# Strips stored by ScalarE, a corner block stored twice, and gate products moved into a loop

## The chip, the cores and the metric

One core of one Trainium2 chip runs the whole kernel. The engines are TensorE (PE in the profile, its weight loads PEld), VectorE (DVE), ScalarE (ACT), GpSimd (POOL) and SyncE (SP, which here only issues DMAs). The metric is the device time of one execution in microseconds, the median of several runs.

## The reference, cut to what matters

One decoder layer on 1024 tokens of width 1024, in float32:

```python
f1 = swiglu(rms_norm(h, ffn1_pre_g), ffn1_w_in, ffn1_w_out)
h = h + 0.5 * rms_norm(f1, ffn1_post_g)
u = rms_norm(h, mix_pre_g)
p_rwkv, p_swa, q_mem, gate_logits = split(u @ w_in)
y_a = rwkv7_mix(p_rwkv, ...)                 # linear recurrence over time, 8 heads of 64
y_b = sliding_window_gqa_sinks(q, k, v, sinks)
y_c = memory_cross_attention(q_mem, mem_n, mem_w_kv)
g = sigmoid(gate_logits + gate_b)            # three gates of width 1024
merged = sum(g_i * (y_i @ w_branch_i))
h = h + rms_norm(merged @ w_out, mix_post_g)
f2 = swiglu(rms_norm(h, ffn2_pre_g), ffn2_w_in, ffn2_w_out)
h = h + 0.5 * rms_norm(f2, ffn2_post_g)
```

The change lies in the middle: in `rwkv7_mix`, whose recurrence runs in chunks of 64 tokens, and in the columns of `u @ w_in` that give the queries, keys and gates.

## The kernel before, in words

Every large product is exact float32 made of three matmuls on split operands (high times high, high times low, low times high; `mm3`, lines 374 to 379). ScalarE casts a weight to its high part (`w_hi`, L300), VectorE subtracts to get the low part (`w_lo`, L302), from a raw tile (`w_raw`) that SP loads (L291). Eight operands are made ahead.

The mixer runs through these stages, each with other work laid between its matmuls:

- **Preparation** (`rwkv_prep`, 700 to 890 us in the profile). For each of four pairs of heads it projects r, k and v, applies the token shift (`raw` tiles, whose first eight columns POOL clears, L970; L965 and L966 mix), and forms the decays. `gram` (L1105) computes, for each half of the sixteen chunks, a 64 by 64 matrix per chunk and head: 128 of them in all. VectorE masks them into a tile `ab` (L1116; one buffer), and SP stores them to `ab_d` (L1118). `ss` and `rk` are sums over a head's channels by matmul (L993).
- **Inverse** (`rwkv_invert`). All 128 matrices are loaded, one per partition, and VectorE inverts the two diagonal 32 by 32 blocks of each; the result goes to `inv_d`, the transpose of one of the blocks to `turn_d`.
- **Pairs of strips** (`win_pair`, L1407). Meanwhile PE computes seven pairs of column strips of `u @ w_in`, each with seven half-size products in place of eight (sums of the operands stand in `mix_form`). Three PSUM banks px, py, pz collect the products. `made` adds a kept sum to a bank and writes half a strip (`att`, L1433; a gate strip's Tanh is L1436). After the seventh product SP stores both strips of 512 KB (L1455): six to `att_d`, eight to `gate_d`.
- **Corner** (`rwkv_corner`, L1167). The off-diagonal 32 by 32 block of each inverse is the product of three blocks: `up` (from `ab_d`), `turned` and `low` (from `inv_d`). SP loads each with four DMAs in pieces of 128 bytes; eight groups of small matmuls (L1185) stand between the products of pairs 4 and 5. ScalarE stores the result into `inv_d` (L1191).
- **Chain** (`rwkv_chain`, L1201). Sixteen chunks in sequence. `f` and `dinv` of a chunk are loaded from `pk_d` and `inv_d` (`chunk_fetch`). In an iteration PE computes z from the state sv, the outputs y, the solution z times dinv, the next chunk's values and gram, the new state and a transpose bkt; VectorE and ScalarE copy between. Products of gate blocks (`pgate`) fill PE's waits. Blocks 10 and 11 (`gate_block`) come whole, the later ones from a generator (`filling`), from which `fill(n, behind)` takes n matmuls that may not start before `behind`.
- **Finish** (`rwkv_finish`). The group norm: for each of eight half-rows a square by ScalarE (`ysq_hi`), its low part by VectorE (`ysq_lo`), a sum by PE (`var`, L1337) and a logarithm by ScalarE (`yrs`), then exponentials. Tanh of the gates needs another table on ScalarE than logarithm and exponential; ACT_TABLE_LOAD switches.

What sets the order on each engine is a scheduler that goes by priorities: `high_priority(offset=...)` moves a group ahead (`lead` 300, `urgent` 1000), `issue_after` holds one back, and `keep_in_program_order` fixes matmuls among themselves. Each engine then runs its own list in order, and a DMA waits in its queue in order as well.

Of the kernel before, what the change touches and what calls it, by code (L numbers as in the profile page):

```python
# [11 lines left out]
F32 = mybir.dt.float32  # L12
# [6 lines left out]
P = 128  # L19
# [19 lines left out]
NPAIR = 4  # L39
# [10 lines left out]
CORNER = (4, 4)  # L50
# [42 lines left out]
class Block:  # L93
# [6 lines left out]
    def mm(self, *args, start=True, stop=True):  # L100
        return self.k.tc.keep_in_program_order(self.nc.tensor.matmul(*args, start=start, stop=stop))
# [130 lines left out]
class Builder:  # L232
# [768 lines left out]

    def rwkv_prep(self, u, pool, pk_d, ab_d, bonus_d, att_d):
        nc = self.nc
# [51 lines left out]
        for p in range(NPAIR):  # L1055
# [49 lines left out]
            def gram(p=p, at=at, bk=bk, bka=bka):  # L1105
                store(bka, 0, p)

                for half in (0, 1):
                    ps = self.psum("ab")
                    for c in range(8):  # L1110

                        for rows, q in heads[::-1]:
                            cc = half * 8 + c
                            keep(nc.tensor.matmul(ps[rows, c * C : (c + 1) * C], bk[q][rows, cc], at[rows, cc], start=True, stop=True))
                    ab = pool.tile([P, 8, C], F32, tag="ab", name="ab", bufs=1)
                    V.tensor_tensor(ab, ps.rearrange("p (c t) -> p c t", t=C), self.gmask[:, 0:1, :].broadcast_to([P, 8, C]), ALU.mult)  # L1116
                    for q in (0, 1):
                        nc.sync.dma_start(ab_d[half * 8 : (half + 1) * 8, p, q].rearrange("c s t -> s c t"), ab[q * 64 : q * 64 + 64])  # L1118

            def bonus(p=p, parts=m_parts, m=m, rv=rv, v=v):  # L1120
# [45 lines left out]

    def rwkv_corner(self, pool, ab_d, inv_d, turn_d):  # L1167

# [5 lines left out]
        with urgent():  # L1174
            for t, d in ((up, flat(ab_d)[:, :H, H:]), (turned, turn_d), (low, flat(inv_d)[:, H:, H:])):
                for g in groups:
                    nc.sync.dma_start(t[g], d[g].rearrange("i s t -> s i t"))
        for w, x, out in ((up, turned, half), (half, low, corner)):
# [22 lines left out]
    def rwkv_chain(self, pool, early, fetched, pk_d, inv_d, y):  # L1201
# [23 lines left out]
        def values(n, ps):  # L1225

            for p, q in pairs:
                mm(at(ps, p, 1 - q, W4), n["f"][ROWS[q], p, 4, :], self.center[ROWS[q]])
            for t in ("sv", "uv"):
                for q in (0, 1):  # L1230
                    S.copy(n[t][ROWS[1 - q], q], v3(ps, W4)[ROWS[1 - q]])

        def grams(n):
# [32 lines left out]
        G.memset(n["sv"][hi, 1], 0.0)  # L1266
        values(n, self.psum("y"))
        grams(n)
# [3 lines left out]
        for c in range(NC_):  # L1272
# [15 lines left out]
            for p, q in pairs:  # L1288
                self.solved = mm(at(ps, p, q, W4), n["d"][ROWS[q], p, :], z[ROWS[q], p, :])
            for q in (0, 1):  # L1290
# [116 lines left out]
    def win_pair(self, i, fs, out, att_d, gate_d, between=lambda: None):  # L1407
# [21 lines left out]
        def made(n, t, h, ps, x=None):  # L1429
            t, f = t[:, halves[h]], strips[n]  # L1430
            with self.tc.high_priority(offset=self.lead):
# [5 lines left out]
                elif x is None:  # L1437
                    nc.scalar.copy(t, ps)

        part(0, "b11", px, True)  # L1440
        x = kept(px)
# [8 lines left out]
        part(5, "b22", pz, False, True)  # L1450
        made(0, first, 1, pz, u1)
        part(6, "t4", px, False, True)
        made(1, second, 0, px)
        for f, t in zip(strips, (first, second)):
            nc.sync.dma_start(gate_d[f - 24] if f >= 24 else att_d[ATT_ROW[f]], t)  # L1455

# [284 lines left out]
    def mixer(self, u, cp, close_raws, att_d, gate_d, km_d, vm_d):  # L1741
        nc, tc, io = self.nc, self.tc, self.io
        pk_d = tc.dram_tile([NC_, P, NPAIR, 5 * C], F32, name="pk_d")
        ab_d = tc.dram_tile([NC_, NPAIR, 2, C, C], F32, name="ab_d")
        inv_d = tc.dram_tile([NC_, NPAIR, 2, C, C], F32, name="inv_d")
        turn_d = tc.dram_tile([P, H, H], F32, name="turn_d")
# [9 lines left out]
        with tc.tile_pool(reuse_waits="tile", name="prep", bufs=8) as pool:  # L1756
            self.rwkv_prep(u, pool, pk_d, ab_d, bonus_d, att_d)
        forms = over.enter_context(tc.tile_pool(reuse_waits="tile", name="mix_forms", bufs=1, side="right"))
# [5 lines left out]
        with tc.tile_pool(reuse_waits="tile", name="gates", bufs=2) as gp:  # L1764
# [17 lines left out]
            with tc.tile_pool(reuse_waits="tile", name="corner", bufs=1) as pool:  # L1782
                lumps = itertools.chain(itertools.repeat(None, CORNER[1]), self.rwkv_corner(pool, ab_d, inv_d, turn_d))
                for i in range(CORNER[0], len(WIN_PAIRS) - 1):
                    self.win_pair(i, fs, out, att_d, gate_d, lambda: next(lumps, None))
                assert next(lumps, None) is None
            chunks = contextlib.ExitStack()
            early = chunks.enter_context(tc.tile_pool(reuse_waits="tile", name="chunks", bufs=2))
            fetched = [self.chunk_fetch(early, c, pk_d, inv_d) for c in (0, 1)]
            self.win_pair(len(WIN_PAIRS) - 1, fs, out, att_d, gate_d)  # L1790
            over.close()
            with chunks, tc.tile_pool(reuse_waits="tile", name="chain", bufs=2) as pool:
                y = pool.tile([P, NPAIR, T], F32, name="y", bufs=1)
                last = self.rwkv_chain(pool, early, fetched, pk_d, inv_d, y)
                for g in range(GATES_FIRST, GATES_EARLY):
                    self.gate_block(g, u, gp, gate_d)
                self.held = []
                self.fills, self.missing = self.filling(u, gp, gate_d, y_d), 0
                self.fill(8, self.solved)
                last()  # L1800
# [267 lines left out]
```

## Time and profile before

| | us |
|---|---|
| median of 3 runs | 2256.76 (2256.03 to 2258.38) |
| profiled execution | 2257.27 |
| its span, first to last instruction | 2255.6 |
| TensorE busy | 2227.7 (99%) |
| VectorE / ScalarE / GpSimd busy | 1642.0 / 1028.9 / 58.8 |
| mean granted TensorE clock | 0.997 |

The stages of the change lie between 760 and 1200 us. In the windows each engine's busy time stands with its count of instructions; a window's length less PE's busy time is PE's idle time there. SP's DMAs are listed by issue, not by transfer; POOL issues no DMA before the change.

### The profile page before, as it was taken

Reading aid. Unit: us, or ns where it says so; the run is one execution under the profiler, and the core shown is the slowest. Engines: PE = TensorE matmul, PEld = TensorE weight load, DVE = VectorE, ACT = ScalarE, POOL = GpSimd, SP = SyncE. Lnnn points to the kernel's source line nnn. Section 1 sums busy time; section 2 is a strip of 40 time slices with the busy share of each in tenths; the row PEclk is TensorE's granted clock in tenths of the full one; section 3 lists DMA queues with packets and bytes.
Section 4 is the critical chain, followed back from the end, with each engine's and each line's share of the span. In section 5 each row is a group of like instructions: output and inputs, shape, how many; then the busy total and the mean of one; then the engine's idle time right before and its main releaser. Section 6 shows DMA issues by size and latency. Waiting matters only on the chain.

```text
span 2255.6 us, 34511 instructions
## 1 busy us (share of the span) xinstructions
PE 2227.7 (99%) x12304; PEld 1832.2 (81%) x12304; DVE 1642.0 (73%) x2761; ACT 1028.9 (46%) x1933; POOL 58.8 (3%) x114
## 2 busy tenths in 40 slices
PE   8999999999999999999999999999999999999998
PEld 6888888888887788877878887788888888888887
DVE  6988767766698887863667577794898886656576
ACT  6523333454556654444355454444663223345451
POOL 0000000000000000000330000000000000000000
PEclk9999999999999999999999999999999999999999
DMA  8565666686665356464538877564565552347663
GB/s 292 174 202 169 202 210 214 229 294 205 191 210 188 120 150 204 155 169 153 158 95 276 270 252 250 185 202 142 174 214 176 194 189 100 114 164 249 205 196 121
DMA packets 279132, 431.90 MB, mean 191 GB/s; under 512 B 58512, under 2 KB 96912, under 8 KB 278704
## 3 DMA queue, kind: packets, MB, share of 16 engines
q1 hardware_dynamic: 266160, 409.96, 56.0%
q10 hardware_dynamic: 12800, 19.73, 2.7%
q8 instruction: 97, 1.59, 0.3%
q14 instruction: 75, 0.61, 0.1%
HBM read 292.75 MB, written 135.79 MB: 190 GB/s over the span
## 4 chain that ended last, share of the span: by engine, by line
PE 51%; DMA 1%; DVE 1%; ACT 1%; issue 0%; SPq 0%; DVEq 0%; ACTq 0%
PE px L377 4%; PE px L379 4%; PE px L378 4%; PE po L377 3%; PE po L378 3%; PE po L379 3%; PE pgate L377 2%; PE pgate L378 2%; PE pgate L379 2%; PE pz L377 2%; PE pz L379 2%; PE pz L378 2%; PE pb L377 2%; PE pb L378 2%; PE pb L379 2%; PE pw L378 1%
## 5 line engine op out<-in xcount | busy, mean ns | idle before, releaser
L300 ACT CAST w_hi<-w_raw 128x512 fp32r<-128x512 f32 x608 | 376.2, 620 | 725.0 <-PE px L378 189.9
L302 DVE TENSOR_TENSOR w_lo<-w_raw,w_hi 128x512 fp32r<-128x512 f32 x608 | 417.3, 688 | 191.0 <-ACT w_hi L300 171.7
L379 PE MATMUL po<-u,w_lo 128*128 128x512 f32 (+1 forms) x476 | 180.9, 380 | 0.0
L378 PE MATMUL po<-u,w_hi 128*128 128x512 f32 (+1 forms) x476 | 180.9, 380 | 0.0
L377 PE MATMUL po<-u,w_hi 128*128 128x512 f32 (+1 forms) x476 | 180.9, 380 | 0.0
L377 PE MATMUL px<-u,w_hi 128*128 128x512 f32 x380 | 147.9, 389 | 0.8 <-DVE km L1596 0.8
L377 PE MATMUL pz<-u,w_hi 128*128 128x512 f32 x380 | 148.1, 390 | 0.0
L378 PE MATMUL px<-u,w_hi 128*128 128x512 f32 x380 | 147.9, 389 | 0.0
L379 PE MATMUL px<-u,w_lo 128*128 128x512 f32 x380 | 147.8, 389 | 0.0
L379 PE MATMUL pz<-u,w_lo 128*128 128x512 f32 x380 | 147.8, 389 | 0.0
L378 PE MATMUL pz<-u,w_hi 128*128 128x512 f32 x380 | 147.8, 389 | 0.0
L377 PE MATMUL px<-f,w_hi 128*128 128x512 f32 x352 | 137.1, 390 | 0.0
L379 PE MATMUL px<-f,w_lo 128*128 128x512 f32 x352 | 137.0, 389 | 0.0
L378 PE MATMUL px<-f,w_hi 128*128 128x512 f32 x352 | 136.9, 389 | 0.0
L486 DVE TENSOR_TENSOR u<-hid,u 128x512 fp32r<-128x512 f32 x114 | 78.3, 690 | 44.7 <-ACT u L485 43.7
L378 PEld LDWEIGHTS po<-u,w_hi 128*128 128x128 f32 x476 | 89.5, 188 | 17.2
L379 PEld LDWEIGHTS po<-u,w_lo 128*128 128x128 f32 x476 | 89.5, 188 | 17.0
L377 PE MATMUL pgate<-u,w_hi 128*128 128x512 f32 x256 | 103.3, 403 | 0.0
L377 PEld LDWEIGHTS po<-u,w_hi 128*128 128x128 f32 x476 | 89.5, 188 | 16.8
L378 PE MATMUL pgate<-u,w_hi 128*128 128x512 f32 x256 | 101.0, 395 | 0.0
L485 ACT CAST u<-hid 128x512 fp32r<-128x512 f32 x114 | 70.6, 620 | 65.0 <-DMA hid<-form_d 54.2
L379 PE MATMUL pgate<-u,w_lo 128*128 128x512 f32 x256 | 100.3, 392 | 0.0
(453 smaller groups left out, 5162.1 us busy)
## 6 DMA issues: line engine op xcount, KB each, us to landing
w_raw<-in_ffn_in SPq DMA_DIRECT2D x224, 256.0 KB
hid<-form_d SPq DMA_DIRECT2D x154, 256.0 KB
w_raw<-in_win SPq DMA_DIRECT2D x112, 256.0 KB
form_d<-g SPq DMA_DIRECT2D x88, 256.0 KB
w_raw<-ffn_sum_d SPq DMA_DIRECT2D x88, 256.0 KB
form_d<-h SPq DMA_DIRECT2D x66, 256.0 KB
w_raw<-in_ffn_out SPq DMA_DIRECT2D x66, 256.0 KB
first_d<-first SPq DMA_DIRECT2D x48, 256.0 KB
```

The lines of the kernel that those rows point to most:

```text
L300: self.nc.scalar.copy(hi, x)
L302: self.split_last = self.nc.vector.tensor_tensor(lo, x, hi.bitcast(F32), ALU.subtract)
L377: mm(out, wh, xh, start=first, stop=False, **kw)
L378: mm(out, wh, xl, start=False, stop=False, **kw)
L379: self.last_mm = mm(out, wl, xh, start=False, stop=last, **kw)
L485: self.nc.scalar.copy(hi, x)
L486: self.nc.vector.tensor_tensor(lo, x, hi.bitcast(F32), ALU.subtract)
```

## The change

- A pair's strips are stored by ScalarE's DMA queue instead of SP's, each as soon as it is complete.
- `gram` stores, besides `ab`, the upper right 32 by 32 block of each matrix to a new buffer `up_d`, laid out by matrix: four DMAs by POOL per pair of heads and half, 32 in all, each 128 pieces of 128 bytes.
- The corner loads `up` by one SP DMA of 128 rows of 4 KB. `turned` stays. `low` comes by eight POOL DMAs, each 512 pieces of 128 bytes.
- The fetch of the first two chunks is urgent.
- Gate blocks 10 and 11 may not start before the first chunk's `values`; `fill` takes 12 matmuls behind the fifth-last solution and 8 behind the last, instead of 8 behind the last.

```diff
@@ rwkv_prep, gram
                     for q in (0, 1):
                         nc.sync.dma_start(ab_d[half * 8 : (half + 1) * 8, p, q].rearrange("c s t -> s c t"), ab[q * 64 : q * 64 + 64])
+                    for q in (0, 1):
+                        for g in (0, 1):
+                            to = up_d[(half * 2 + g) * H : (half * 2 + g + 1) * H, p * 2 + q :: 2 * NPAIR, :]
+                            nc.gpsimd.dma_start(to, ab[q * 64 : q * 64 + H, g * 4 : g * 4 + 4, H:])
@@ rwkv_corner
-            for t, d in ((up, flat(ab_d)[:, :H, H:]), (turned, turn_d), (low, flat(inv_d)[:, H:, H:])):
-                for g in groups:
-                    nc.sync.dma_start(t[g], d[g].rearrange("i s t -> s i t"))
+            nc.sync.dma_start(up, up_d)
+            for g in groups:
+                nc.sync.dma_start(turned[g], turn_d[g].rearrange("i s t -> s i t"))
+            for g in groups:
+                for a in (0, H // 2):
+                    nc.gpsimd.dma_start(low[g, a : a + H // 2], flat(inv_d)[g, H:, H:][a : a + H // 2].rearrange("i s t -> s i t"))
@@ rwkv_chain
-        values(n, self.psum("y"))
+        self.opened = values(n, self.psum("y"))
+        self.solved = []
...
-                self.solved = mm(at(ps, p, q, W4), n["d"][ROWS[q], p, :], z[ROWS[q], p, :])
+                solved = mm(at(ps, p, q, W4), n["d"][ROWS[q], p, :], z[ROWS[q], p, :])
+            self.solved.append(solved)
@@ win_pair
+        def stored(n, t):
+            f = strips[n]
+            with self.tc.high_priority(offset=self.lead):
+                nc.scalar.dma_start(gate_d[f - 24] if f >= 24 else att_d[ATT_ROW[f]], t)
...
         made(0, first, 1, pz, u1)
+        stored(0, first)
         part(6, "t4", px, False, True)
         made(1, second, 0, px)
-        for f, t in zip(strips, (first, second)):
-            nc.sync.dma_start(gate_d[f - 24] if f >= 24 else att_d[ATT_ROW[f]], t)
+        stored(1, second)
@@ mixer
-            fetched = [self.chunk_fetch(early, c, pk_d, inv_d) for c in (0, 1)]
+            with tc.high_priority(offset=self.urgent):
+                fetched = [self.chunk_fetch(early, c, pk_d, inv_d) for c in (0, 1)]
...
-                for g in range(GATES_FIRST, GATES_EARLY):
-                    self.gate_block(g, u, gp, gate_d)
+                with tc.issue_after(self.opened.ins):
+                    for g in range(GATES_FIRST, GATES_EARLY):
+                        self.gate_block(g, u, gp, gate_d)
...
-                self.fill(8, self.solved)
+                self.fill(12, self.solved[-5])
+                self.fill(8, self.solved[-1])
```

How the change moves instructions is seen in the lists of three engines (row number, line, operation, out<-in and shape; the line numbers after the change are some ten higher). First VectorE in the fourth pair of strips, around the first corner group. Before:

```order
1103 L302 TENSOR_TENSOR w_lo<-w_raw,w_hi 128x512 x3
1104 L1433 TENSOR_TENSOR att<-pz,part 128x512
1105 L302 TENSOR_TENSOR w_lo<-w_raw,w_hi 128x512
1106 L327 TENSOR_TENSOR part<-w_raw 128x512
1107 L328 TENSOR_TENSOR w_raw<-w_raw 128x512
1108 L329 TENSOR_TENSOR w_raw<-part,w_raw 128x512
1109 L1433 TENSOR_TENSOR att<-px,part 128x512
```

With the change:

```order
1103 L302 TENSOR_TENSOR w_lo<-w_raw,w_hi 128x512
1104 L1443 TENSOR_TENSOR att<-px,part 128x512
1105 L302 TENSOR_TENSOR w_lo<-w_raw,w_hi 128x512 x2
1106 L327 TENSOR_TENSOR part<-w_raw 128x512
1107 L328 TENSOR_TENSOR w_raw<-w_raw 128x512
1108 L1443 TENSOR_TENSOR att<-pz,part 128x512
1109 L302 TENSOR_TENSOR w_lo<-w_raw,w_hi 128x512
1110 L329 TENSOR_TENSOR w_raw<-part,w_raw 128x512
```

The addition that reads px stood last and now stands ahead of the one that reads pz. Next TensorE in the last two iterations of the chain. Before:

```order
4607 L1211 MATMUL z<-uv,bk 64x64 x8
4608 L1250 MATMUL bkt<-ident,f 128x128 x4
4609 L378 MATMUL pgate<-u,w_hi 128x512
4610 L379 MATMUL pgate<-u,w_lo 128x512
4611 L1211 MATMUL z<-sv,gz 64x64 x8
...
4617 L1211 MATMUL z<-uv,bk 64x64 x8
4618 L1250 MATMUL bkt<-ident,f 128x128 x4
4619 L1211 MATMUL z<-sv,gz 64x64 x8
```

With the change, the last of them:

```order
4614 L1218 MATMUL z<-uv,bk 64x64 x8
4615 L1258 MATMUL bkt<-ident,f 128x128 x4
4616 L378 MATMUL pgate<-u,w_hi 128x512
4617 L379 MATMUL pgate<-u,w_lo 128x512
4618 L377 MATMUL pgate<-u,w_hi 128x512
4619 L378 MATMUL pgate<-u,w_hi 128x512
4620 L379 MATMUL pgate<-u,w_lo 128x512
4621 L377 MATMUL pgate<-u,w_hi 128x512
4622 L1218 MATMUL z<-sv,gz 64x64 x8
```

Between bkt and the next z stand six gate products now, as in the iterations before. Last ScalarE in the finish, where before no table load stands between the first square and the exponentials. With the change:

```order
788 L1349 ACTIVATE yrs<-var,gn_eps 128x512
789 L300 CAST w_hi<-w_raw 128x512
790 L1483 ACT_TABLE_LOAD
791 L1483 ACTIVATE gate<-pgate,half_gb 128x512
792 L1336 ACTIVATE ysq_hi<-y 128x512
793 L1349 ACT_TABLE_LOAD
794 L1349 ACTIVATE yrs<-var,gn_eps 128x512
795 L1336 ACTIVATE ysq_hi<-y 128x512
...
801 L1483 ACT_TABLE_LOAD
802 L1483 ACTIVATE gate<-pgate,half_gb 128x512
803 L300 CAST w_hi<-w_raw 128x512
804 L1349 ACT_TABLE_LOAD
```

Two gate activations of a later block have moved in between the logarithms, and each brings two table loads with it.

On POOL the 32 stores stand among the clearings of the raw tiles, and the eight loads of `low` behind them. On SP, behind the store of the inverse, stand one load of `up`, four of `turned`, eight of raw weights, then the first two chunks' f and dinv, then five raw weights.

More of the change, by code (lines that the diff above doesn't have):

```diff
@@ L1000, in chunked, with rwkv_prep @@
         return x.rearrange("p (c t) -> p c t", t=C) if len(like.shape) == 3 else x
-    def rwkv_prep(self, u, pool, pk_d, ab_d, bonus_d, att_d):
+    def rwkv_prep(self, u, pool, pk_d, ab_d, up_d, bonus_d, att_d):
         nc = self.nc
@@ L1165, in rwkv_invert, with rwkv_corner @@
         nc.sync.dma_start(turn_d, turned)
-    def rwkv_corner(self, pool, ab_d, inv_d, turn_d):
+    def rwkv_corner(self, pool, up_d, inv_d, turn_d):
         nc = self.nc
@@ L1227, in values @@
             for p, q in pairs:
-                mm(at(ps, p, 1 - q, W4), n["f"][ROWS[q], p, 4, :], self.center[ROWS[q]])
+                valued = mm(at(ps, p, 1 - q, W4), n["f"][ROWS[q], p, 4, :], self.center[ROWS[q]])
             for t in ("sv", "uv"):
@@ L1231, in values @@
                     S.copy(n[t][ROWS[1 - q], q], v3(ps, W4)[ROWS[1 - q]])
+            return valued
         def grams(n):
@@ L1744, in mixer @@
         ab_d = tc.dram_tile([NC_, NPAIR, 2, C, C], F32, name="ab_d")
+        up_d = tc.dram_tile([P, H, H], F32, name="up_d")
         inv_d = tc.dram_tile([NC_, NPAIR, 2, C, C], F32, name="inv_d")
@@ L1756, in mixer @@
         with tc.tile_pool(reuse_waits="tile", name="prep", bufs=8) as pool:
-            self.rwkv_prep(u, pool, pk_d, ab_d, bonus_d, att_d)
+            self.rwkv_prep(u, pool, pk_d, ab_d, up_d, bonus_d, att_d)
         forms = over.enter_context(tc.tile_pool(reuse_waits="tile", name="mix_forms", bufs=1, side="right"))
@@ L1782, in mixer @@
             with tc.tile_pool(reuse_waits="tile", name="corner", bufs=1) as pool:
-                lumps = itertools.chain(itertools.repeat(None, CORNER[1]), self.rwkv_corner(pool, ab_d, inv_d, turn_d))
+                lumps = itertools.chain(itertools.repeat(None, CORNER[1]), self.rwkv_corner(pool, up_d, inv_d, turn_d))
                 for i in range(CORNER[0], len(WIN_PAIRS) - 1):
```

## The prediction, made before the changed kernel was run

> **What bounds the kernel now.** I read the page's busy times first, then the windows, then the list of waits of TensorE (PE) from 700 to 1200, then the timeline around each wait (start and length in us, engine, line, operation, count, and in brackets the idle time before it and who ended it). The first fence holds a row of the page, three windows and four waits:
>
> ```profile
> PE 2227.7 (99%) x12304; PEld 1832.2 (81%) x12304; DVE 1642.0 (73%) x2761; ACT 1028.9 (46%) x1933; POOL 58.8 (3%) x114
> 900.00:1000.00 100.00, 100.00 (x442) 82.81 (x442) 84.37 (x152) 43.66 (x73) 0.00 (x0) 1.00 0.48 163
> 1000.00:1050.00 50.00, 46.64 (x681) 37.15 (x680) 15.57 (x24) 18.19 (x31) 0.00 (x0) 0.97 0.52 127
> 1150.00:1200.00 50.00, 47.17 (x485) 38.17 (x486) 35.54 (x62) 30.24 (x53) 15.53 (x17) 1.00 0.31 98
> PE px L377 <- DVE att L1433: 3.4, 1, 3.4
> PE z L1211 <- DVE sv L1302: 1.8, 2, 1.1
> PE ss L993 <- DVE n_lo L486: 1.3, 1, 1.3
> PE var L1337 <- DVE ysq_lo L1327: 0.8, 1, 0.8
> ```
>
> PE sets the end: it is busy 99%. No edit takes work from PE (its matmuls are the same, some in other places), so the change can win only PE's waits in the stages that it touches, and lose by new ones. The window rows show these waits, as the window's length less PE's busy time: none in 900 to 1000, 3.4 us in 1000 to 1050, 2.8 in 1150 to 1200. The wait rows name them. The largest is one wait of 3.4 us in the pair of strips whose time holds the first corner products (rows of SP, DVE and PE):
>
> ```profile
> 991.75 0.41 SPq L1455 DMA_DIRECT2D gate_d<-att  x1
> 992.25 5.49 SPq L1177 DMA_DIRECT2D iup<-ab_d  x4
> 1004.03 0.69 DVE L302 TENSOR_TENSOR w_lo<-w_raw,w_hi 128x512 fp32r<-128x512 f32 x1 [2.03 <-ACT w_hi L300]
> 1006.13 0.39 PE L377 MATMUL px<-u,w_hi 128*128 128x512 f32 x1
> 1012.68 0.69 DVE L1433 TENSOR_TENSOR att<-pz,part 128x512 f32<-128x512 f32 x1 [2.47 <-PE pz L379]
> 1015.94 0.68 DVE L1433 TENSOR_TENSOR att<-px,part 128x512 f32<-128x512 f32 x1
> 1016.68 0.65 PE L377 MATMUL px<-mix_form,w_hi 128*128 128x512 f32 x1 [3.36 <-DVE att L1433]
> 1020.43 0.39 PE L377 MATMUL px<-mix_form,w_hi 128*128 128x512 f32 x1
> ```
>
> The last product of the pair adds into px, and may not start before DVE has read px in att<-px. What att<-px reads was complete when PE went on to the next pair's first product at 1006.13. Yet it ran at 1015.94: it stands in DVE's order behind att<-pz, which had to wait for pz until 1012.68, and behind a w_lo and three operations on raw weights (four operations in the 2.6 us between). After the wait PE is slow as well: nine matmuls take 1020.43 - 1016.68 = 3.75 us, where nine at the usual pitch of 0.228 us take 2.05. So the place costs 3.36 + 1.70 = 5.06 us.
>
> **The change part by part.** *Corner loads, strip stores, urgent fetches* (one answer: they act through the order of the queues). What wins here is DVE's new order, in which att<-px stands ahead of att<-pz, right behind the w_lo of 1004.03. It can run at about 1006.5, six microseconds before PE asks for it (at 1016.68 - 3.36 = 1013.3). I take the whole 5.06 us as won. att<-pz now stands behind two operations on raw weights; their loads go out earlier too, since SP has one iup in place of four (5.49 us) and no ilow (four of about 0.9) ahead of them, and pz is not written again before the next pair's fourth product. The lower end is 0, if something else holds PE at that place. PE has no idle time in 900 to 1000, so that the strips' stores leave SP gains nothing there. On ScalarE (ACT) the 14 stores cost some 0.4 us of issue each, as the 991.75 row: 5.7 us on an engine 46% busy, hidden by its idle time. In SP's order the f and dinv of chunks 0 and 1 now stand ahead of five w_raw, and dinv waits for the corner's store. Operands are made eight products ahead (2.7 us each), which covers a w_raw some 2 us late; nothing.
>
> *ilow by GpSimd (POOL).* Eight transfers of 512 pieces; none of POOL's DMAs is in this trace. POOL is empty then, and the price is on whoever waits:
>
> ```profile
> 1025.36 0.75 PE L1185 MATMUL corner<-ilow,ihalf 32*32 32x32 f32 x64
> L1177 SPq DMA_DIRECT2D iup<-ab_d x4: 382/899/3160, 992.2 to 997.2; - x4
> L1177 SPq DMA_DIRECT2D ilow<-inv_d x4: 777/896/992, 1001.4 to 1004.3; - x4
> ```
>
> The loads can start when inv_d is stored, which I estimate at 993, since SP's first load of the corner went at 992.25 (above). The first ilow matmul moves up by 5.06 to 1020.3 and needs seven of eight. With a landing of 2.8 us (below) each may take (27.3 - 2.8) / 7 = 3.5 us. SP's rows take 0.78 to 0.99 for twice the pieces: below the limit by a factor of 3.5. I take nothing; at 4.2 us each PE would wait about 5 us.
>
> *up_d, the block stored twice.* Per pair of heads and half, four POOL DMAs read ab. ab has one buffer, so DVE's next ab waits for them. The intervals between the end of one ab and the next, within a pair:
>
> ```profile
> 767.60 0.68 DVE L1116 TENSOR_TENSOR ab<-ab,gmask 128x512 f32<-128x512 f32 x1
> 778.26 0.68 DVE L1116 TENSOR_TENSOR ab<-ab,gmask 128x512 f32<-128x512 f32 x1
> 800.82 0.69 DVE L1116 TENSOR_TENSOR ab<-ab,gmask 128x512 f32<-128x512 f32 x1
> 806.49 0.58 SPq L1118 DMA_DIRECT2D ab_d<-ab  x1
> 809.84 0.69 DVE L1116 TENSOR_TENSOR ab<-ab,gmask 128x512 f32<-128x512 f32 x1 [0.43 <-DMA ab_d<-ab]
> 814.92 0.69 DVE L302 TENSOR_TENSOR w_lo<-w_raw,w_hi 128x512 fp32r<-128x512 f32 x1 [0.64 <-ACT w_hi L300]
> 837.89 0.69 DVE L1116 TENSOR_TENSOR ab<-ab,gmask 128x512 f32<-128x512 f32 x1
> 844.19 0.68 DVE L1116 TENSOR_TENSOR ab<-ab,gmask 128x512 f32<-128x512 f32 x1
> 847.31 0.69 DVE L302 TENSOR_TENSOR w_lo<-w_raw,w_hi 128x512 fp32r<-128x512 f32 x1 [1.84 <-ACT w_hi L300]
> 872.42 0.68 DVE L1116 TENSOR_TENSOR ab<-ab,gmask 128x512 f32<-128x512 f32 x1
> 882.25 0.68 DVE L1116 TENSOR_TENSOR ab<-ab,gmask 128x512 f32<-128x512 f32 x1
> 884.36 0.69 DVE L302 TENSOR_TENSOR w_lo<-w_raw,w_hi 128x512 fp32r<-128x512 f32 x1 [1.43 <-ACT w_hi L300]
> L1118 SPq DMA_DIRECT2D ab_d<-ab x16: 580/628/3757, 770.3 to 885.8; - x16
> ```
>
> They are 9.98, 8.33, 5.61 and 9.15 us. Landing takes 2.8 us: SP's issue ended at 807.07, and the waiting ab came at 809.84. With c us for each POOL DMA, four need 4c + 2.8. Bounds of c: below, SP's 0.58 for a store of this tile with four times the pieces (5.1 us: no wait); above, the longest issue of corner pieces, iup's 3.16, taken as 3. I take 0.9, since iup's and ilow's medians on SP are for the same 128-byte pieces: 6.4 us, 0.8 late in the third pair alone, and the 1.84 us idle at 847.31 absorbs it. Nothing. If c is larger, what ab is late is covered by DVE's next idle time: nothing in the first pair (the 1.3 us wait of ss hangs on the operation right behind that ab), 0.64 us in the second, 1.84 in the third, 1.43 in the fourth; the rest I charge to PE in full, a bound, since PE's lead over DVE isn't counted. At c = 2 that is 0.8 + 1.8 + 3.4 + 0.2 = 6.2 us, at 1.93 some 5.2, at 3 some 22.
>
> The POOL's small memsets of raw stand behind these DMAs; the one for the second pair's r moves behind its eight, yet its reader is 13 us later. They bind from c of about 3.
>
> *The trap.* The trace shows that POOL and DVE can hinder each other: w_lo takes 1.18 us instead of 0.69 beside POOL's squares.
>
> ```profile
> 1183.08 1.18 DVE L302 TENSOR_TENSOR w_lo<-w_raw,w_hi 128x512 fp32r<-128x512 f32 x1 [0.26 <-ACT w_hi L300]
> 768.20 0.68 DVE L1043 TENSOR_SCALAR sz<-sz 128x1024 f32<-128x1024 f32 x1
> ```
>
> The Trainium skill, "SBUF — State Buffer", section "SBUF: two separate sides", speaks against the change: POOL's DMAs are written by its own cores, which cannot write while DVE runs a mode that takes both ports; about 620 ns alone, about 3100 ns beside such an operation. By 620 ns the stores would cost nothing; by 3100 for all of them about 24 us, an estimate from that page. Behind the first ab stands one candidate, the 0.68 us row above, so I give the rule its chance in the slow rival below.
>
> *Gate products in the loop.* The two early blocks and the fills give each of the fifteen iterations six products, where the last two before had 2 and 0:
>
> ```profile
> 1159.05 0.69 PE L1211 MATMUL z<-sv,gz 128*64 128x64 f32 x16 [0.79 <-DVE sv L1302]
> 1165.56 0.69 PE L1211 MATMUL z<-sv,gz 128*64 128x64 f32 x16 [1.05 <-DVE sv L1302]
> ```
>
> The list of waits has z waiting twice in all, and these are the two: the iterations with six before them have none. 1.8 us won.
>
> *The finish.* ACT's new order has gate's Tanh and table loads between the logarithms. Ahead of the sixth square stand two loads and one gate.
>
> ```profile
> 1172.42 1.28 ACT L1330 ACT_TABLE_LOAD   x1
> 1180.24 0.63 ACT L1326 ACTIVATE ysq_hi<-y 128x512 fp32r<-128x512 f32 x1 [1.35 <-PE var L1337]
> 1181.35 0.62 ACT L1326 ACTIVATE ysq_hi<-y 128x512 fp32r<-128x512 f32 x1
> 1182.61 0.40 PE L1337 MATMUL var<-ysq_hi,bones_r 128*128 128x512 f32 x1
> ```
>
> That is 2 x 1.28 + 0.6, and 0.6 for a weight's cast that moved ahead as well, less the 1.35 us that ACT idles there: 2.4 us. The square ends near 1184.4 instead of 1182.0, and its low part by DVE near 1185, so PE, which comes for them at 1182.61 and 1182.9, loses about 2.3 us; the 0.80 behind is then covered. Net 1.5 lost. Bounds: 0.5 (one load hidden), and 4 (all four loads and both gates, 6.4, less that idle time and the 0.80).
>
> Sum: -5.06 - 1.8 + 1.5 = -5.4 us (5.36). The profiled execution took 2257.27 us (span 2255.6), 0.5 above the median of 2256.76. From the median: **2251.4 us**.
>
> **The rivals.** *POOL's DMAs are slow (slower).* If each takes 2.3 us, ab is late by 2.0, 3.7, 6.4 and 2.85; less the covers 2.0 + 3.0 + 4.6 + 1.4 = 11.0 us: 2256.8 - 5.4 + 11.0 = 2262.4. It decides from c of about 1.95, where the gain is eaten. For it: no row bounds a POOL DMA; against it: 128 pieces are few.
>
> *A transfer or an order takes the wait's place (same).* If ilow needs 4.2 us each, PE waits 5 at the second corner product and the 5.06 are spent there; the same sum comes out if the change doesn't do what its first part says, because something else holds PE where px waited. Then -1.8 + 1.5: 2256.5. Against it: SP's issue rows, and the six microseconds att<-px has in hand.
>
> *The finish costs more (same).* With the upper bound of 4 the sum is -2.9: 2253.9.
>
> **How the numbers follow.** The measurement tells about 0.2%, 4.5 us. Forecast 0.56 (its own range 2249.2 to 2253: 1 less for a finish that costs 0.5, 1.5 more for one that costs 3, and a microsecond for waits that shift by themselves), transfer or order 0.15, finish 0.14, slow POOL 0.15. Faster by over 0.2% (under 2252.3) is the forecast without its uppermost part: 0.54; within: 0.32, the two middle cases and a little of the slow one; slower: 0.14. The range 2248.5 to 2260.5 holds all but the worst of the slow rival and a little below.
>
> **What would show it.** Right: no wait of px around 1013 and att<-px near 1006.5; no wait of z in the loop; a wait of 2 us on var; the ab of the third pair within 1 us of 844; POOL's up_d issues near 0.9 us. Wrong: ab waiting for up_d by several us and PE waiting on ss or ab in 770 to 890; corner waiting for ilow; px waiting as before.

## The result and the profile after

| | before | after |
|---|---|---|
| median, nine runs each (us) | 2256.76 (2255.29 to 2260.35) | 2263.46 (2260.17 to 2266.86) |
| ratio | | 1.0026, 95% interval 1.0016 to 1.0037 |
| profiled execution / its span | 2257.27 / 2255.6 | 2261.35 / 2259.3 |

The kernel became slower by 0.26%, where 2251.4 was forecast and faster by over 0.2% held the larger chance. The time lies 3 us above the range. The profiled execution of the changed kernel is the third fastest of the nine, so its trace shows a difference of 4.1 us where the medians differ by 6.7.

Some of these 4.1 us come before the stages of the change. TensorE's last product of the queries ahead of the pairs of strips, before (first fence) and after (second; start, length and operation):

```profile
894.38 0.39 PE L379 MATMUL pq<-u,w_lo 128*128 128x512 f32 x1
```

```profile
896.44 0.39 PE L379 MATMUL pq<-u,w_lo 128*128 128x512 f32 x1
```

The after run is 2.1 us late there, and 2.0 of them were lost before 750, ahead of the first store of up_d. 1.4 lie at the very start, where the program is the same: the first 56 matmuls began 0.32 us later and took 1.09 longer. Places in the trace of after at the pairs of strips are to be read with these 2.1 us taken off. What is left of the span's 3.7 us is 1.6 us from the pairs of strips and the stages behind them.

These 1.6 us are the sum of large terms of both signs. The windows of TensorE after (length, busy time and instructions of PE, PEld, DVE, ACT and POOL, granted clock, DMA share, GB/s), and the one window of before that the prediction did not look at:

```profile
1000.00:1050.00 50.00, 50.00 (x700) 39.62 (x700) 19.33 (x29) 21.02 (x35) 4.58 (x7) 1.00 0.56 160
...
1200.00:1230.00 30.00, 25.72 (x108) 20.91 (x107) 20.35 (x29) 4.23 (x8) 1.00 (x2) 0.94 0.76 265
```

```profile
1200.00:1230.00 30.00, 30.00 (x134) 24.88 (x133) 22.23 (x34) 11.06 (x20) 1.96 (x3) 1.00 0.94 314
```

In 1000 to 1050 TensorE was idle for 3.4 us at a clock of 0.97; now it is busy throughout at 1.00. In 1200 to 1230, which lies behind the stage that the prediction treated as the last one, it was busy throughout; now it is idle for 4.3 us at 0.94. The list of TensorE's waits after names the stalls (total, count, longest):

```profile
PE msc L101 <- DMA vm_in<-vm_d: 4.3, 1, 4.3
PE var L1347 <- ACT ysq_hi L1336: 1.2, 1, 1.2
PE px L377 <- ACT part L1436: 1.0, 1, 1.0
PE var L1347 <- DVE ysq_lo L1337: 0.5, 2, 0.3
```

The wait of px for att (3.4) and both waits of z (1.8) are gone. New are a wait of `msc`, the first scores of the attention behind the finish, 1.2 on var, and 1.0 of px in the last pair of strips. (A wait for several transfers is put down to the one that came last by the profile; which load msc waited for is seen below.)

**The corner.** VectorE in the fourth pair after:

```profile
1008.47 0.69 DVE L1443 TENSOR_TENSOR att<-px,part 128x512 f32<-128x512 f32 x1 [1.65 <-PE px L379]
...
1015.53 0.69 DVE L1443 TENSOR_TENSOR att<-pz,part 128x512 f32<-128x512 f32 x1 [1.10 <-PE pz L379]
```

att<-px now stands ahead of att<-pz, and runs as soon as px is complete: 1008.47, or 1006.4 without the late start, where the prediction put it at 1006.5.

TensorE's order has changed here as well. The first group of corner products, one piece before (first fence), goes in three pieces after, with products of px between them:

```profile
1008.94 0.75 PE L1185 MATMUL corner<-iturned,iup 32*32 32x32 f32 x64
```

```profile
1008.31 0.25 PE L1192 MATMUL corner<-iturned,iup 32*32 32x32 f32 x4
1009.85 0.24 PE L1192 MATMUL corner<-iturned,iup 32*32 32x32 f32 x2
1011.84 0.70 PE L1192 MATMUL corner<-iturned,iup 32*32 32x32 f32 x58
```

From the last product of px (1005.90 before, 1007.99 after) to the second corner group (1012.57 and 1015.42) TensorE runs the same matmuls without a wait, in 6.67 us before and 7.43 after. So 0.76 of the 5.06 us are given back.

**The finish.** ScalarE between the last copy of y and the end of the exponentials (squares, casts and most logarithms left out):

```profile
1171.89 1.28 ACT L1340 ACT_TABLE_LOAD   x1
...
1178.89 1.28 ACT L1483 ACT_TABLE_LOAD   x1
1180.18 0.69 ACT L1483 ACTIVATE gate<-pgate,half_gb 128x512 f32<-128x512 f32 x1
...
1181.40 1.28 ACT L1349 ACT_TABLE_LOAD   x1
...
1186.70 1.28 ACT L1483 ACT_TABLE_LOAD   x1
...
1189.38 1.28 ACT L1349 ACT_TABLE_LOAD   x1
1190.68 1.26 ACT L1349 ACTIVATE yrs<-var,gn_eps 128x512 f32<-128x512 f32 x2
1191.96 1.28 ACT L1353 ACT_TABLE_LOAD   x1
1193.26 2.96 ACT L1353 ACTIVATE yrs<-yrs 128x1024 f32<-128x1024 f32 x3
```

Two gates' Tanh (1180.18, and one behind the load at 1186.70) stand between the logarithms, with five table loads behind the first. Before, one load at 1172.42 served logarithms and exponentials alike:

```profile
1187.50 3.89 ACT L1343 ACTIVATE yrs<-yrs 128x1024 f32<-128x1024 f32 x4
```

From the first table load to the first exponential it was 1187.50 - 1172.42 = 15.1 us, and is 1193.26 - 1171.89 = 21.4: the exponentials are 6.3 us late. SP's queue shows what hangs on them, before and after:

```profile
1203.84 3.25 SPq L1362 DMA_DIRECT2D y_d<-yrs  x4
1209.32 0.92 SPq L191 DMA_DIRECT2D qm<-att_d  x2
1210.28 1.72 SPq L1810 DMA_DIRECT2D km_in<-km_d  x1
```

```profile
1206.07 5.63 SPq L1372 DMA_DIRECT2D y_d<-yrs  x4
1216.04 0.93 SPq L191 DMA_DIRECT2D qm<-att_d  x2
1217.55 0.43 SPq L1829 DMA_DIRECT2D km_in<-km_d  x1
SPq L191 <- DMA y_d<-yrs: 3.5, 1, 3.5
```

(The last row is from the list of SP's waits.) The results y are stored after the exponentials; `qm`, the first load of the attention behind it, waits for these stores to land (3.5 us; before 0.2), as its tile takes the place of the finish's tiles; `km_in` and `vm_in` stand behind `qm` in SP's queue. The issue of km_in ends at 1217.98 instead of 1212.00, and TensorE's scores multiply qm and km_in. TensorE before and after:

```profile
1219.46 1.89 PE L101 MATMUL msc<-km_in,qm 128*128 128x256 f32 x8
```

```profile
1224.57 3.46 PE L101 MATMUL msc<-km_in,qm 128*128 128x256 f32 x8 [4.28 <-DMA vm_in<-vm_d]
```

The trace names vm_in as the releaser, but that is not the load that held msc: by the semaphore records of the trace km_in is complete at 1224.01 and vm_in only at 1226.00, when msc, which doesn't read it, already runs. Before, km_in was complete at 1217.20 and msc came for it at 1219.46. So 2.3 us of slack hid this load, and nothing on the way showed it as a wait. The stall costs 4.28 us, and the eight matmuls behind it take 3.46 us instead of 1.89: together 5.85, more than the corner's 5.06.

### The profile page after: what moved, and what is told of

Same layout as the page of the kernel before. It is cut to its first block, busy times and chain, and to the rows that moved or that the text cites. A ratio compares the mean times of both kernels' runs of the same rounds, so it can differ in the third digit from the quotient of the medians.

```text
span 2259.3 us, 34577 instructions
## 1 busy us (share of the span) xinstructions
PE 2229.2 (99%) x12304; PEld 1832.0 (81%) x12304; DVE 1641.6 (73%) x2761; ACT 1032.3 (46%) x1935; POOL 80.1 (4%) x154
## 4 chain that ended last, share of the span: by engine, by line
PE 90%; DVE 4%; DMA 3%; ACT 2%; issue 1%; SPq 0%; ACTq 0%; DVEq 0%
PE px L377 9%; PE px L379 9%; PE px L378 9%; PE po L377 6%; PE po L378 6%; PE po L379 6%; PE pz L377 4%; PE pz L379 4%; PE pz L378 4%; PE pgate L377 2%; PE pgate L378 2%; PE pgate L379 2%; PE pr L377 2%; PE pr L378 2%; PE pr L379 2%; PE pb L377 2%
```

## The experiments

Each kernel is the kernel after with one edit, or the kernel before with one part alone, as its diff says. The ratio is to the kernel before on the same chip, whose medians were 2256.3 to 2256.5. Two accounts stood against each other at first: that the gate products in the loop cause the loss, by way of ScalarE's table loads in the finish; or that the new transfers of GpSimd (32 stores of up_d, eight loads of ilow) do.

### The gate products: undone, and alone

Undone (e1_no_loop; against the kernel after):

```diff
-        self.opened = values(n, self.psum("y"))
+        values(n, self.psum("y"))
...
-                with tc.issue_after(self.opened.ins):
-                    for g in range(GATES_FIRST, GATES_EARLY):
-                        self.gate_block(g, u, gp, gate_d)
+                for g in range(GATES_FIRST, GATES_EARLY):
+                    self.gate_block(g, u, gp, gate_d)
...
-                self.fill(12, self.solved[-5])
-                self.fill(8, self.solved[-1])
+                self.fill(8, self.solved)
```

> The changed kernel with its loop part undone (gate blocks 10 and 11 and the fills as before; stores, up_d, ilow and urgent fetches kept). Theory A (the loop part lost the time: it moves two gate activations with their table loads between the logarithms of the finish, the exponentials come 5.8 us later, with them the stores of y, the loads of km and vm queued behind these on SP, and msc waits 4.3 us): no wait of msc on vm_in, var waits under 1 us, no wait of px on ACT's copy, z waits 1.8 us again, and the corner's 5.06 us stay won: 2256.8 - 5 = 2251.8, within 1.5. Theory B (the POOL transfers or the stores on ScalarE lost it): time stays near 2262.

Measured: 2251.92 (2250.79 to 2255.24, eleven runs), ratio 0.9981 (0.9972 to 0.9990). Its list of TensorE's waits between 900 and 1240 is

```profile
PE var L1345 <- DVE ysq_lo L1335: 0.8, 1, 0.8
PE bkt L1258 <- ACT uv L1238: 0.6, 1, 0.6
PE z L1218 <- DVE sv L1310: 0.6, 1, 0.6
PE z L1218 <- DVE z L1290: 0.2, 1, 0.2
```

and nothing else: neither px nor msc waits. z waits 0.8 in all, not 1.8, though the loop's part is undone: in the order that the other edits give, the loop's part had less to win than the trace of before says.

The same part alone, on the kernel before (e2_loop_alone): what the diff ahead takes out, put in, and nothing else.

```diff
-                for g in range(GATES_FIRST, GATES_EARLY):
-                    self.gate_block(g, u, gp, gate_d)
+                with tc.issue_after(self.opened.ins):
+                    for g in range(GATES_FIRST, GATES_EARLY):
+                        self.gate_block(g, u, gp, gate_d)
...
-                self.fill(8, self.solved)
+                self.fill(12, self.solved[-5])
+                self.fill(8, self.solved[-1])
```

> The kernel before with the loop part alone. Theory A: exponentials late, msc waits 3 to 6 us, z no longer waits, px waits for att as before (3.4 us): 2256.8 - 1.8 + 0.9 + 1.4 + 5.8 = 2263, within 2. Theory B: 2255 to 2257, as the waits of z go and little comes for them.

Measured: 2265.44 (2263.81 to 2269.65, five runs), ratio 1.0042 (1.0030 to 1.0055), slightly above what was expected. Its waits are msc 3.8, px on att 3.4 as before, px in the last pair 1.6, var 1.7, and in the attention pv 1.3 and ptr 0.4; the trace is of the slowest of the five runs. So the loop's part costs some 9 us by itself, and about as much on top of the others.

### One half of the loop's part at a time

Only the two gate blocks held until the chain has opened (e5_opened_only; against after):

```diff
-                self.fill(12, self.solved[-5])
                 self.fill(8, self.solved[-1])
```

> The changed kernel without its fill of 12 (8 behind the last solution, as before); the two gate blocks still start behind the first values. Theory A1 (the fill of 12 does the harm: with it a gate block is complete 12 products earlier, so its Tanh falls between the logarithms): no table load there, no wait of msc, nearly no wait of z, px still waits 1.0 us for ACT's copy: 2251.9 (the kernel without the loop part) - 1.4 + 1.0 to 1.5 = 2251.5 to 2252. Theory A2 (moving the blocks out of the last pair does it): 2261 to 2263.

Only the fill of twelve (e6_fill_only; against after):

```diff
-                with tc.issue_after(self.opened.ins):
-                    for g in range(GATES_FIRST, GATES_EARLY):
-                        self.gate_block(g, u, gp, gate_d)
+                for g in range(GATES_FIRST, GATES_EARLY):
+                    self.gate_block(g, u, gp, gate_d)
```

> The changed kernel with its fill of 12, but the two gate blocks free to start in the last pair as before. Theory A1: four table loads around two gates between the logarithms, msc waits 3 to 5 us, px doesn't wait: 2263.5 - 1.2 = 2262. Theory A2: 2252.

Measured: 2252.70 (ratio 0.9982, 0.9972 to 0.9991) for the blocks, 2260.07 (ratio 1.0019, 1.0010 to 1.0028) for the fill, 2 us below what was expected. The waits of TensorE with the blocks alone, then with the fill alone:

```profile
PE px L377 <- ACT part L1436: 1.0, 1, 1.0
PE var L1347 <- DVE ysq_lo L1337: 0.8, 1, 0.8
```

```profile
PE msc L101 <- DMA w_raw<-in_win: 3.8, 1, 3.8
PE var L1347 <- ACT ysq_hi L1336: 1.2, 1, 1.2
```

The blocks win the waits of z (none is left) and lose 1.0 at px: these gate products used to stand in the last pair of strips, and covered this wait there. The fill of twelve alone brings the wait of msc (here a w_raw is named; km_in is issued at 1217.08, nearly as late as after, and is complete at 1223.09, and msc starts at 1223.65). With twelve products spent behind the fifth-last solution, the gate blocks are complete earlier, and their Tanh falls between the logarithms.

### GpSimd's stores of up_d undone

e4_up_undone; the 32 stores left out, `up` loaded by four SP DMAs from ab_d as before (the call, not shown, passes ab_d under the name up_d):

```diff
-                    for q in (0, 1):
-                        for g in (0, 1):
-                            to = up_d[(half * 2 + g) * H : (half * 2 + g + 1) * H, p * 2 + q :: 2 * NPAIR, :]
-                            nc.gpsimd.dma_start(to, ab[q * 64 : q * 64 + H, g * 4 : g * 4 + 4, H:])
...
-            nc.sync.dma_start(up, up_d)
+            for g in groups:
+                nc.sync.dma_start(up[g], flat(up_d)[g, :H, H:].rearrange("i s t -> s i t"))
```

> The changed kernel without the 32 POOL stores; up comes from ab_d by four SP loads of 128-byte pieces as before. Theory A: 2263, within 1, since ab waits for none of these stores by more than 0.8 us in the profile after. Theory B: 2257 or less.

Measured: 2260.99 (2258.39 to 2266.12), ratio 1.0023 (1.0013 to 1.0032); msc waits 3.8. This is 1 us below the expected 2262 to 2264, yet by the ratios the kernel is as slow as the kernel after to within the intervals. The stores of up_d are not what loses the time. The eight loads of ilow stand in e1 too, which is fast. So the second account falls.

### The late exponentials: taken away, and made by other means

The held gates only behind the last exponential (e3_gates_late; against after, whose fills stay):

```diff
-            keep(S.activation(rs[:, p], rs[:, p], ACT.Exp, scale=-0.5))
+            rooted = keep(S.activation(rs[:, p], rs[:, p], ACT.Exp, scale=-0.5))
...
-        for f in held:
-            f()
+        with self.tc.issue_after(rooted.ins):
+            for f in held:
+                f()
```

> The changed kernel with one line more: the gate activations that the finish holds back may not be issued before the last exponential, so that no table load stands between the logarithms. Theory A: the exponentials start near 1187 to 1188, var waits under 1 us, msc's wait on vm_in goes: 2263.5 - 4.3 - 1.5 (slow clock behind the wait) - 1 = 2256.7 or less. If the gates' banks are then freed too late, a wait of pgate on gate of 1 to 2 us comes instead. Theory B: 2263, unchanged.

Measured: 2257.74 (2253.02 to 2262.99), ratio 1.0003 (0.9994 to 1.0012). No table load stands between the logarithms, the exponentials run from 1184.41, var waits 0.3, and msc still waits 1.6 us:

```profile
1205.46 0.75 DVE L1367 SCALAR_TENSOR_TENSOR yrs<-yrs,vecs,bo_in 128x512 f32<-128x512 f32 x1 [2.48 <-DMA bo_in<-bonus_d]
```

The last y now waits for another load, `bo_in`, which the new order puts late in SP's queue, and y_d, qm and km_in stand behind it as before (km_in is complete at 1217.58, and msc starts at 1218.14). The median is a microsecond above the expected time. The eleven runs fall into two groups, 2253.0 to 2255.3 (four) and 2257.7 to 2263.0 (seven), and the trace (2253.90) is of the first.

To see whether that load holds what is left, it was put ahead too (e7_gates_bo; against e3_gates_late):

```diff
-            nc.sync.dma_start(bo, bonus_d[p][:, cols])
+            with self.tc.high_priority(offset=self.lead):
+                nc.sync.dma_start(bo, bonus_d[p][:, cols])
```

> The changed kernel with the gates held behind the last exponential, as in the run before, and the loads of the bonus (bo_in) ahead by the lead that operands have. Theory E (what was left there, 5.8 us above the kernel without the loop part, is again the lateness of the y stores, now by a bo_in load that came last in SP's order and 2.5 us late): the last y store goes 3 us earlier, msc doesn't wait, and the px wait of 1.0 and ptr's 0.4 stay: 2252.5 to 2254. Otherwise 2257.7, unchanged.

Measured: 2257.66 (2253.70 to 2259.22), ratio 1.0001 (0.9992 to 1.0010). A miss. In the profiled execution (2254.03) the wait of msc is gone, yet the median is that of e3. Its eleven runs fall into two groups, 2253.7 to 2256.4 and 2257.7 to 2259.2, and the profile is from the first. A wait of pv for sc (1.3 us) in the attention is new. What costs the second group its 4 us, here and in e3, was not seen in any trace.

The other way round: e1's order, in which the finish is as before, with ten needless exponentials ahead of its own (e8_late_exp; against e1_no_loop). Nothing reads their results.

```diff
+        spare = fin("spare")
+        for _ in range(10):
+            keep(S.activation(spare, rs[:, 3, TH:], ACT.Exp, scale=-0.5))
...
-        for f in held:
-            f()
+        with self.tc.issue_after(rooted.ins):
+            for f in held:
+                f()
```

> The changed kernel without its loop part, and with ten needless exponentials of 128x512 (0.57 us each) ahead of the finish's four, no table load added; gates held behind the last exponential. Theory A (late exponentials alone make msc wait for the loads of km and vm): msc waits 3 to 5 us, the clock behind it is low for some 3 us, time 2251.9 + 5.8 = 2257.7, within 1.5. If instead the table loads or the earlier products do it in some other way: 2252 to 2253, var and msc without new waits.

Measured: 2265.82 (2263.60 to 2268.82, five runs), ratio 1.0043 (1.0030 to 1.0056). The exponentials start at 1191.60, 9.0 us behind those of e1 (1182.62). TensorE's new waits:

```profile
PE sc L101 <- DVE pt L169: 4.3, 1, 4.3
PE msc L101 <- DMA vm_in<-vm_d: 4.2, 1, 4.2
PE pgate L377 <- ACT gate L1485: 1.8, 1, 1.8
```

Late exponentials, without a gate among the logarithms and with the loop as before, bring the same wait of msc: km_in is complete at 1223.98, and msc starts at 1224.54. They don't come quite alone. This kernel also holds the gates back, and one of its last results y waits 1.8 us for bo_in, as in e3. There that lateness left msc a wait of 1.6 us with the exponentials in time, so most of the 4.2 is theirs, but not surely all. The size of the time was missed, since the two other waits, 6.1 us, were not foreseen. The one of pgate, at 1198, is of the gates that this kernel itself holds back. The one of sc is in the attention, at 1400; whether the late exponentials cause it too was not tried.

### What wins: the stores of the strips

The stores alone, on the kernel before (e9_stores_alone):

```diff
+        def stored(n, t):
+            f = strips[n]
+            with self.tc.high_priority(offset=self.lead):
+                nc.scalar.dma_start(gate_d[f - 24] if f >= 24 else att_d[ATT_ROW[f]], t)
...
-        for f, t in zip(strips, (first, second)):
-            nc.sync.dma_start(gate_d[f - 24] if f >= 24 else att_d[ATT_ROW[f]], t)
```

> The kernel before with the strips' stores on ScalarE alone; corner loads, up_d and loop as before. Its list on VectorE already has att<-px ahead of att<-pz. Theory C (the corner's gain comes from the stores leaving SP, by the order that follows): no wait of px, 2256.5 - 5.06 = 2251.5, within 1. Theory D (the corner's loads on POOL and the second copy of the block are what wins): the wait of 3.4 us stays or ilow's late loads take its place, 2256 to 2257.

Measured: 2250.90 (2249.49 to 2255.54, eleven runs), ratio 0.9979 (0.9970 to 0.9987). This is the fastest kernel of the study, faster than both. VectorE's order is the one of the kernel after, and TensorE's window is full:

```profile
1007.64 0.69 DVE L1433 TENSOR_TENSOR att<-px,part 128x512 f32<-128x512 f32 x1 [1.66 <-PE px L379]
1013.93 0.69 DVE L1433 TENSOR_TENSOR att<-pz,part 128x512 f32<-128x512 f32 x1 [2.47 <-PE pz L379]
1000.00:1050.00 50.00, 50.00 (x703) 39.92 (x702) 18.90 (x29) 20.81 (x35) 0.00 (x0) 1.00 0.59 153
```

The stores in SP's queue again, the other edits of the corner kept (e11_no_stores; against e1_no_loop). One account has the stores carry the gain, the other the corner's loads:

```diff
-                nc.scalar.dma_start(gate_d[f - 24] if f >= 24 else att_d[ATT_ROW[f]], t)
+                pass
...
-        stored(1, second)
+        for f, t in zip(strips, (first, second)):
+            nc.sync.dma_start(gate_d[f - 24] if f >= 24 else att_d[ATT_ROW[f]], t)
```

> The changed kernel without its loop part and with the strips' stores on SP as before: only up_d, ilow on POOL and the urgent fetches are left. VectorE's list has att<-px behind att<-pz again, without the operations on raw weights between. Theory C (the stores' place is what wins): px waits 1 to 1.5 us (att<-pz ends at 1013.3, a w_lo and att<-px follow), with some slow clock behind it: 2253 to 2255.5. Theory D (corner loads win): 2251.9, as with the stores on ScalarE.

Measured: 2261.54 (2260.88 to 2263.14, nine runs), ratio 1.0025 (1.0015 to 1.0035).

```profile
PE z L1218 <- DVE sv L1310: 7.1, 6, 1.3
PE px L377 <- DVE att L1441: 2.0, 1, 2.0
```

px waits for att again, so it is the stores that win it. The edit does two things at once, however: it moves the stores to another queue, and puts each where its strip is complete, at a higher priority. Which of the two brings VectorE's order was not tried. The size was missed: without the stores the order of this kernel has six waits of z in the loop, 7.1 us, and the edits of the corner lose 5 us. With the stores they cost nothing that can be told (e1 at 0.9981 against e9 at 0.9979).

The stores, the fill of twelve, the gates behind the exponentials and bo_in ahead (e10_stores_tail; against e9):

```diff
-                self.fill(8, self.solved)
+                self.fill(12, self.solved[-5])
+                self.fill(8, self.solved[-1])
...
-        for f in held:
-            f()
+        with self.tc.issue_after(rooted.ins):
+            for f in held:
+                f()
...
-            nc.sync.dma_start(bo, bonus_d[p][:, cols])
+            with self.tc.high_priority(offset=self.lead):
+                nc.sync.dma_start(bo, bonus_d[p][:, cols])
```

> The kernel before with the stores on ScalarE, the fill of 12, the gates held behind the last exponential and bo_in ahead; gate blocks free to start in the last pair; corner loads as before. Theory E: no wait of px, z or msc; the stores alone took 2250.9 and still waited 1.5 us on z and bkt: 2249.5 to 2250.5. If the loads of km and vm are late for another reason, msc waits 1 to 2 us: 2252 to 2255.

Measured: 2252.16 (2250.28 to 2255.11), ratio 0.9983 (0.9974 to 0.9991). A miss by some 2 us: no wait of px on att, of z or of msc is left, but pv waits 1.1 us for sc and ptr 0.4 in the attention, which e9 has not. The 1.3 us won at z are given back there.

## Why the prediction was wrong, step by step

| Term | predicted (us) | in the trace after (us) |
|---|---|---|
| corner: wait of px, slow clock | -5.06 | -5.06 |
| corner: first group in three pieces | not looked at | +0.76 |
| loop: two waits of z | -1.8 | -1.8 |
| finish: var | +1.5 | 1.2 + 0.5 - 0.8 = +0.9 |
| last pair: px | 0 | +1.0 |
| behind the finish: msc, and slow clock | not looked at | 4.28 + 1.57 = +5.85 |
| attention: sc<-pt, 0.8 before, gone | not looked at | -0.8 |
| sum | -5.4 | +0.9 |

The first and third entries of the last column are waits and slow matmuls of the trace before that the trace after no longer has.

- **Right: the corner, less 0.8.** The wait went and no other wait took its place there; TensorE's new order around the corner's first group, which the step did not look at, costs 0.76. The rival in which ilow or another transfer takes it over did not come. The step left open which edit does it; e9 and e11 say the stores.
- **Right: GpSimd's transfers cost nothing; wrong: the price of an ilow.** The views of the two lines that issue up_d and ilow (length least, median, most; first and last start; count), and of the line that writes ab:

```profile
L1122 POOL DMA_DIRECT2D up_d<-ab x32: 520/522/709, 770.6 to 887.1; - x32
DMA to landing us min/median/max: 1.9/3.7/7.8
L1184 POOL DMA_DIRECT2D ilow<-inv_d x8: 648/656/678, 993.7 to 1020.6; - x8
DMA to landing us min/median/max: 2.3/3.2/7.1
  DMA ab_d<-ab: 0.8, 1
```

  An up_d takes 0.52 us, below the 0.9 assumed. ab waits once for ab_d, 0.8 us (before: 0.4), and not for up_d. The Trainium skill's "SBUF — State Buffer", section "SBUF: two separate sides", gives some 3100 ns for such a transfer beside a copy by VectorE against 620 alone. No issue of this trace took over 709 ns; whether VectorE ran an operation of the kind that the page means beside them, the trace does not tell. Either way the rival of slow transfers falls, since ab never waited for up_d, and e4 shows no cost of the stores beyond its interval. For ilow the price was wrong: from the first start to the seventh's end it is 3.4 us each, not 0.9. That nothing came of it was luck rather than working, as the step's own limit was 3.5.
- **Right in sign, worth less: the loop.** z has no wait after. But e1, without this part, has 0.8 us of it left, and e5, with the blocks alone, pays 1.0 at px for the rest; the medians of e1 and e5 are the same to within the intervals. The step gave no price to the place that the gate blocks leave: in the last pair they had covered 1.0 us.
- **Wrong: the finish.** The mechanism at var was right (a wait of 1.2 and two of 0.25 and 0.28; 2.3 forecast). The failing step is where the working stopped. Its upper bound names "all four loads and both gates, 6.4"; the exponentials are in fact 6.3 us late, with five loads, the fifth for the exponentials themselves. But this was priced only at the next matmul that waits for ScalarE, var. What the exponentials feed is y, its stores, and through SP's queue the loads of the next stage. The prediction never asked what is late next behind the exponentials; in the trace of before those rows were there to read (y_d at 1203.84, km_in at 1210.28, msc at 1219.46), with no wait of msc, since 2.3 us of slack were enough. The chain is supported from three sides: e6 brings it by the fill alone, e8 brings the same wait of msc by exponentials made late in another way (with a smaller lateness of bo_in beside them), and e3 has the exponentials in time and a shorter wait, for another reason that also acts through y_d and SP's queue.
- **The rival of a dearer finish** had the right place. It stopped at the bound of 4 and forecast 2253.9, as it did not leave the stage.

In the traces the sum is then +0.9, where the spans, less the late start, differ by +1.6. Small waits that the table leaves out account for the rest to within 0.2 us: ptr in the attention, 0.4, and po behind 2000, 0.3, both new, and 0.3 more of ps_rs behind 2000 (the other part of its rise, from 1.1 to 1.7, lies before 894 and belongs to the late start).

Not accounted for is the difference between the profiled executions (4.1) and the medians (6.7): the eight other runs of the kernel after have no trace. What they do show is their mean granted clock. The profiled run had 0.998, the run at the median 0.996, the slowest (2266.86) 0.995. A clock lower by 0.002 over 2229 us of TensorE's work is worth up to 4.5 us, an estimate, so it may be the clock. The trace of e2 shows one way: right behind its waits of var the granted clock falls (0.66 from 1188 to 1193), where the traced run of after, with the same waits, kept 1.00. That is argued, not shown: no run changed the clock alone.

What stays open: the second group of the runs of e3 and e7, and why the waits of pv come up in e2, e7 and e10. In e7 the clocks, 0.997 and 0.998 against 0.998, do not tell the groups apart clearly.

## What to carry to other kernels

When an engine that is off the path becomes late, follow its last result and not its next reader only: here the exponentials' delay ran through a store, a tile whose place the next stage takes over, and the loads behind it in one queue, to a matmul 31 us later that had shown no wait. Price each place from which work is taken, as well as the one it goes to; the gate products had covered a wait where they stood. And where an edit has several parts, try each alone: one move of fourteen stores to another queue held the whole gain (-5.4 us), and one fill of twelve products more than spent it.

## What the runs showed of the hardware

- A table load takes 1.28 us each time. Before, no load stood between the logarithms and the exponentials behind them (one at 1172.42 served both); after two Tanh among the logarithms a load stood ahead of the exponentials too (1191.96), though logarithms stood right before it.
- GpSimd issues 128 pieces in 0.52 us and 512 in 0.66, so four times the pieces cost a quarter more. But its eight issues of ilow do not follow each other: 2.0 to 6.8 us lie between them, named "issue" by the trace, and the eight took 27.5 us from the start of the first (993.7) to the end of the last (1020.6 + 0.65). TensorE did not wait for them:

```profile
993.70 0.68 POOL L1184 DMA_DIRECT2D ilow<-inv_d  x1 [106.05 <-ACT att L1446]
1001.18 0.66 POOL L1184 DMA_DIRECT2D ilow<-inv_d  x1 [6.79 <-issue]
...
1016.99 0.66 POOL L1184 DMA_DIRECT2D ilow<-inv_d  x1 [2.72 <-issue]
```

  The corner needs seven of them, and the seventh has been issued at 1017.65, 24.0 us behind the first start: 3.4 us each. The prediction assumed some 0.9 from SP's rows and gave 3.5 as the limit from which the corner waits. The first product that reads ilow went at 1023.21, 5.6 us behind that issue, and an ilow took 2.3 to 7.1 us to land. So this edit came far closer to a loss than its working said.
- After an idle stretch of 4.28 us TensorE ran eight matmuls in 3.46 us instead of 1.89. The window shows the granted clock at one half there; behind the wait of 3.36 us before, it is 0.51 from 1016.8 to 1020.3:

```profile
1224.20:1227.60 3.40, 3.03 (x7) 2.52 (x8) 0.69 (x1) 0.00 (x0) 0.00 (x0) 0.50 0.71 271
```

  In the kernels with such a wait the mean granted clock of the runs is 0.995 to 0.998 (after, e2, e4, e6, e8), in those without it 0.997 to 0.999 (e1, e5, e10; e9 with one run at 0.996). The two ranges overlap.
